# Two conv projections of a hybrid decoder layer as seven-product pairs behind attention

## The chip, the cores and the metric

One core of a Trainium2 chip runs the whole layer in one launch. The metric is device time in microseconds of that core; three runs of the kernel before gave 1265.51, 1268.23 and 1270.88 us. PE is the matmul engine (PEld its weight loads), DVE the vector engine, ACT the scalar engine, POOL is GpSimd, SP the engine that mostly issues transfers.

## The reference

One layer, 1024 positions of width 1024. `B`, `C`, `xc` are called cb, cc, cx in the kernel, 512 columns each; the gates are ga and gc, 1024 columns each.

```python
proj = h @ w_in[l]
q, k, v, cb, cc, cx, g_att, g_conv = jnp.split(proj, IN_SPLITS, axis=-1)
o = stick_breaking_attention(heads(q), heads(k), heads(v))
y_att = o.transpose(0, 2, 1, 3).reshape(b, s, ATT_WIDTH) @ w_att_branch[l]
y_conv = (cb * causal_dwconv(cc * cx, conv_mix_w[l])) @ w_conv_branch[l]
merged = jax.nn.sigmoid(g_att) * y_att + jax.nn.sigmoid(g_conv) * y_conv
x = x + rms_norm(merged @ w_out[l], norm_mix_post[l])
h = rms_norm(x, norm_ffn_pre[l])
u = causal_dwconv(h @ w_up[l], conv_ffn_w[l])
a, g = jnp.split(u, 2, axis=-1)
f = (jax.nn.gelu(g, approximate=True) * a) @ w_down[l]
x = x + rms_norm(f, norm_ffn_post[l])
```

Attention has 8 heads of 64. Its weight for query t and key s is sigmoid(z[t,s]) times the product of 1 - sigmoid(z[t,j]) for s < j < t, so each row needs a scan over the keys between the two matrix products.

## The kernel before, in words

**Numbers.** A float32 operand is held as two fp16 tiles, hi and lo, under a power-of-two scale. A product takes three matmuls (hi x hi, hi x lo, lo x hi; PASSES) for every 128 rows of depth. ACT makes the hi part (L102, L550), DVE the lo part (L103, L551). A scale needs a sum over all of the tile: squares on ACT (L63), a one-column matmul `pr` with ones on PE (L81, L475), and a few tiny DVE instructions.

**The first half of the run** is ordered by a planner (class Plan, L1826). Every piece of work is a job with engine, cost, the buffers it reads and writes, and a due time; the planner writes out an order for each of PE, DVE, ACT, SP and POOL. PE's backbone are the fills (list FILL, L33): v, then the projections q, k, cb, cc, cx (4 tiles of 128 columns each; 192 matmuls of 512 columns for each of the five), the first gate tiles ga0 and gc0, and four half-tiles of the conv branch (`branch_fill`). Attention work is put between pieces of the fills. Weights of a fill are loaded by POOL (L543), in buffers `ws`, and split into `wh`.

**Attention** is 48 units: per pair of heads j = 0 to 3 three groups of four units, two diagonal ones (keys and queries in the same half of the positions) and one that is not. A unit: z = q k (PE, L757, buffer z: 2), sigmoid into e (ACT, L778, buffer e: 3), two scans (DVE, L785), hi part of the weight w (ACT, L799, buffer w: 2), lo part (DVE, L805/L808), and two transposes of w into wt (SP, L796, hi and lo). After four units, eight transposes, `weigh` makes o = wt v on PE (24 matmuls, also L757). wt has one buffer, so the transposes of a group wait until o of the group before has read it. The names below are `z2_113`: pair of heads 2, query half 1, key half 1, block 3.

**Conv.** `conv_fill` evicts cc to u (ACT), multiplies u by cx on eviction (DVE, L690), takes the three taps (ACT L695, DVE L697), multiplies by cb (DVE, L690) and sums squares. `p_parts` splits the result p into p16 (L709, L710). All of it is a part of the plan, beside attention.

**Behind the plan** another scheduler keeps the order of the code on each engine, apart from a few evictions raised in priority. `branch` makes the conv branch y_conv tiles ywc (from p16 and wc) and the attention branch tiles ywa (from o16 and wa), 24 matmuls per tile of 128 columns (L886). `blocks(q)` makes sums and differences of the four quarters of h (T1 to T4, L919, L921, L923) and splits them into hB and a part of hT (`halves`, L909 on ACT, L910 on DVE). They feed the pairs: two weight tiles multiplied with h by seven block products instead of eight (class Pair; a product is 4 k x 3 matmuls, so 84 for two tiles where plain projection takes 96). `pair_fetch` loads the two tiles (SP, L119), `pair_sums` and `pair_split` form the weight combinations (L1060 to L1062, L1075) and split them into four `wh` tiles (L102, L103). Gate pairs g1 to g7 run so (L1954), with `merge_m` (L941, L943) multiplying gates and branches into m, and `split_m` splitting m under a scale that needs the sums of all 16 branch tiles (known at d = 3). Then come the out-projection (py, L1208) and the ffn (pu L1407, pq L1566, pd L1636 and L1669).

## Time and profile before

| | |
|---|---|
| runs | 1265.51, 1268.23 (median), 1270.88 us |
| profiled execution | 1263.36 us, span of its instructions 1261.6 us |
| granted PE clock | 0.998 |
| moved by the DMA engines | 152.43 MB |
| stages by the start of their first instruction on PE | o of the first group 72.1, last o 332.4, first gate pair 426.0, out-projection 554.4 us |

The profile is of one execution. A row by line gives line, engine, operation, output<-inputs by the program's names (buffer numbers left out), count, busy time, mean duration in ns, and the idle time of the engine ahead of it with what ended it. A matmul's duration runs from issue to end, and matmuls overlap, so the price of one is read from a stretch of them. A wait is put down to the instruction that ended it.

### The profile page before, as it was taken

The numbers are of one execution on the slowest core, as the hardware profiler recorded it, in microseconds if no ns is written. First come the engines' busy times: TensorE is split into PE (matmuls) and PEld (weight loads), VectorE is DVE, ScalarE is ACT, GpSimd is POOL, SyncE is SP. The second block draws the span as 40 slices with busy tenths as digits, with TensorE's granted clock in tenths as the row PEclk, the third lists the DMA queues.
The fourth block names the chain that finished last, engine by engine and source line by source line (L and its number), as shares of the span: only waits on it lengthen the run. The fifth ranks groups of instructions, "written<-read, shape, count | busy, mean of one in ns | idle before, by whom it ended". The sixth has DMA issues, their size and how long they took to land.

```text
span 1261.6 us, 16604 instructions
## 1 busy us (share of the span) xinstructions
PE 1244.5 (99%) x6120; PEld 562.6 (45%) x6120; DVE 1030.1 (82%) x1661; ACT 836.8 (66%) x1215; POOL 99.1 (8%) x137
## 2 busy tenths in 40 slices
PE   9999999999999999999999999999999999999997
PEld 4444444444444444444444444444444444444443
DVE  7977787468729658888889999799799979969976
ACT  7665666346559657765566759768876977878424
POOL 1200000000000000001100001001200300111003
PEclk9999999999999999999999999999999999999999
DMA  8854665535502113414952304614930971594608
GB/s 277 190 136 102 133 131 105 101 76 100 125 2 67 67 34 133 168 68 104 229 156 76 126 21 171 229 34 71 240 124 2 179 222 34 83 248 157 180 1 134
DMA packets 146628, 152.43 MB, mean 121 GB/s; under 512 B 114169, under 2 KB 114297, under 8 KB 146546
## 3 DMA queue, kind: packets, MB, share of 16 engines
q1 hardware_dynamic: 132720, 102.07, 29.7%
q0 software_dynamic: 13824, 49.29, 17.6%
q8 instruction: 48, 0.79, 0.3%
q14 instruction: 34, 0.28, 0.1%
q10 hardware_dynamic: 2, 0.00, 0.0%
HBM read 84.49 MB, written 37.75 MB: 97 GB/s over the span
## 4 chain that ended last, share of the span: by engine, by line
PE 45%; DVE 2%; DMA 1%; ACT 1%; issue 1%; POOL 1%; POOLq 0%; DVEq 0%; ACTq 0%
PE pq L1566 12%; PE pd L1636 2%; PE pd L1669 1%; DMA hB<-n 1%; PE pu7b L1407 1%; PE pu10b L1407 1%; PE pu9b L1407 1%; PE pu2b L1407 1%; PE pu20b L1407 1%; PE pu17b L1407 1%; PE pu15b L1407 1%; PE pu13b L1407 1%; PE pu6b L1407 1%; PE pu4b L1407 1%; PE pu21b L1407 1%
## 5 line engine op out<-in xcount | busy, mean ns | idle before, releaser
L1407 PEld LDWEIGHTS <-wh_u 128*128 128x128 f16 x1848 | 179.2, 98 | 218.6 <-issue 2.1
L1954 PEld LDWEIGHTS <-wh_g 128*128 128x128 f16 x588 | 56.9, 98 | 68.4
L1157 DVE SCALAR_TENSOR_TENSOR wh_u<-ws_u,sc_u,wh_u 128x1024 f16<-128x1024 f32 (+1 forms) x66 | 72.2, 1103 | 15.3 <-ACT wh_u L1155 14.7
L1155 ACT ACTIVATE wh_u<-ws_u,sc_u 128x1024 f16<-128x1024 f32 (+1 forms) x66 | 66.3, 1006 | 26.9 <-DVE sc_u L1140 5.5
L1208 PE MATMUL py<-wh_wo,m 128*128 128x512 f16 x384 | 83.6, 379 | 0.0
L1570 ACT ACTIVATE st<-pq,sd 128x512 f32<-128x512 f32 x112 | 73.6, 698 | 9.8 <-DVE ua L1450 5.6
L1121 POOL DMA_DIRECT2D acc<-st x56 | 43.9, 783 | 427.3 <-ACT st L1570 427.3
L63 ACT ACTIVATE jk_u<-ws_u 128x1024 bf16<-128x1024 f32 x44 | 46.3, 1052 | 22.7 <-DMA ws_u<-w_up_nt 22.4
L799 ACT ACTIVATE w<-e 128x1024 f16<-128x1024 f32 (+3 forms) x48 | 40.1, 837 | 31.6 <-DMA wt<-w 30.7
L1208 PEld LDWEIGHTS <-m 128*128 128x128 f16 x384 | 37.4, 98 | 44.9
L1439 DVE SCALAR_TENSOR_TENSOR ua<-ca,cw_a,ua 128x1023 f32<-128x1023 f32 (+1 forms) x44 | 56.2, 1278 | 1.2 <-ACT ua L1437 1.1
L1439 DVE SCALAR_TENSOR_TENSOR ug<-cg,cw_g,ug 128x1023 f32<-128x1023 f32 (+1 forms) x44 | 56.2, 1278 | 0.1
L778 ACT ACTIVATE e<-z,cz 128x1024 f32<-128x1024 f32 (+3 forms) x48 | 42.3, 896 | 21.0 <-PE z L757 10.5
L785 DVE TENSOR_TENSOR_SCAN e<-e,mask 128x512 f32<-128x512 f32 (+3 forms) x64 | 49.3, 810 | 5.6 <-ACT e L778 5.5
L564 PE MATMUL pq<-hT,wh_q 128*128 128x512 f16 x192 | 42.8, 379 | 1.4 <-DMA hT<-x 1.4
L564 PE MATMUL pcc<-hT,wh_cc 128*128 128x512 f16 x192 | 43.8, 379 | 0.0
L564 PE MATMUL pk<-hT,wh_k 128*128 128x512 f16 x192 | 43.7, 379 | 0.0
L564 PE MATMUL pcb<-hT,wh_cb 128*128 128x512 f16 x192 | 43.7, 379 | 0.0
L564 PE MATMUL pcx<-hT,wh_cx 128*128 128x512 f16 x192 | 43.6, 379 | 0.0
L785 DVE TENSOR_TENSOR_SCAN e<-e,cr,mask 128x512 f32<-128x512 f32 x32 | 39.6, 1271 | 4.1 <-ACT e L778 4.1
L1566 PE MATMUL pq<-wq,fx 128*128 128x512 f16 x192 | 42.8, 379 | 0.0
L1566 PE MATMUL pq<-wq,fy 128*128 128x512 f16 x192 | 42.7, 379 | 0.0
(733 smaller groups left out, 2750.6 us busy)
## 6 DMA issues: line engine op xcount, KB each, us to landing
acc<-st POOLq DMA_DIRECT2D x56, 512.0 KB, 5.9
ws_u<-w_up_nt SPq DMA_DIRECT2D x44, 512.0 KB, 3.8
ds<-w_down SPq DMA_DIRECT2D x22, 512.0 KB, 10.8
ws_g<-w_in_nt SPq DMA_DIRECT2D x14, 512.0 KB, 3.6
x<-x SPq DMA_DIRECT2D x8, 512.0 KB, 8.5
ws_wo<-w_out SPq DMA_DIRECT2D x8, 512.0 KB, 5.9
xr<-x SPq DMA_DIRECT2D x8, 512.0 KB, 4.2
yacc<-acc SPq DMA_DIRECT2D x16, 256.0 KB, 11.2
```

The costliest lines, as they stand in the source:

```text
L63: self.nc.scalar.activation(self.junk(f"jk_{name}"), src, AF.Square, accum_out=acc)
L564: pe.matmul(ps.t, w.t[:, wi, ds(k * P, P)], hT[:, hi, k, ds(c * NH, NH)], start=k == 0 and p == 0, stop=k == KD - 1 and p == 2)
L785: vec.tensor_tensor_scan(x, x, m[:, ::-1], ONE if diag else cr.t[:, h:h + 1], ALU.mult, ALU.max)
L1121: j = pl.add(eng, 0.45 if eng == "SP" else 1.14, lambda: e.dma_start(dst(), srcf(), **kw), r, [b] if w is None else w, ahead=AHEAD["load"] ...
L1155: A(C["As" if big else "Ash"], lambda: act.activation(dst.t[:, 0, dsl], src.t[:, ssl], AF.Copy, scale=sb.t["s"]), [(src, sreg), sb], [(dst ...
L1157: V(C["V" if big else "Vh"], lambda: vec.scalar_tensor_tensor(dst.t[:, 1, dsl], src.t[:, ssl], sb.t["s"], dst.t[:, 0, dsl], ALU.mult, ALU. ...
L1208: pe.matmul(b.t, m16[k].t[:, h_, ds(tt * P, P)], wo[k].t[:, w_, sl], start=k == 0 and p == 0, stop=k == 7 and p == 2)
L1407: pe.matmul(b.t, p.w[wt].t[:, wi, ds(wc * NH + k * P, P)], pr.block(i, h, k), start=first and n == 0, stop=n == 3 * KH - 1, skip_group_che ...
L1439: V(C["V"], lambda lag=lag: vec.scalar_tensor_tensor(u.t[:, lag:], c.t[:, :T - lag], sm.t[:, 2 - lag:3 - lag], u.t[:, lag:], ALU.mult, ALU ...
L1566: pe.matmul(b.t, fa[p].t[:, h, ds(fo * NH + tt * P, P)], wa[p].t[:, x, ds(wo * NH, NH)], start=first and n == 0, stop=n == 5, skip_group_c ...
L1570: A(C["Ah"], lambda tt=tt, b=b, st=st: act.activation(st.t[:, tt % 2, :], b.t, AF.Copy, scale=q.sd.t[:, 0:1]), [b, q.sd], [(st, str(tt % 2 ...
L1954: nc.tensor.matmul(ps, w[wt][:, wi, ds(wc * NH + k * P, P)], self.block(i, hi, k), start=first and n == 0, stop=n == 3 * KH - 1, skip_grou ...
```

## The change

- FILL keeps q, k, cc and the first gate tiles. cx and cb leave the plan and become four pairs x0, x1, b0, b1 (class Conv) of seven products each, between the attention branch and the gate pairs. `conv_taps` and `conv_gate` do what `conv_fill` did, on whole tiles of 1024 columns; `p_split` follows b1 at d = 1.
- All four wa tiles are loaded and split inside the plan; the eight wa branch tiles follow the plan at once, with blocks(0) ahead of them and blocks(1) after the fourth. T4 goes into hT at once.
- The wc tiles are loaded by POOL inside the plan for the sums of their squares only (one scale for all four) and loaded again by SP later; the wc branch tiles stand behind the first four gate pairs, two at each.
- The scale of m takes a bound for the wc part (from the scales of p and wc) in place of the sums of ywc, so m is split inside `merge` from d = 1.
- In attention, the weights w of even blocks t lie in the general slab (`slot`), those of odd t in the two old buffers: four in all.
- Of the units, those with c = 1 may start two fills later (4 + START).

```diff
-FILL = ("q0 k0 q1 k1 cc0 cx0 q2 k2 cb0 cc1 cx1 cb1 cc2 cx2 q3 k3 cb2 cc3 cx3 cb3 ga0 gc0").split()
+FILL = "q1 k1 cc0 q2 k2 q3 k3 cc1 cc2 cc3 ga0 gc0".split()
...
+        self.psrc.update({f"{n}{i}": [win[b + 2 * i], win[b + 2 * i + 1]] for n, b in (("x", 16), ("b", 8)) for i in range(2)})
...
-                    def conv_fill(j, which):
...
+                    def cc_fill(j):
+                        w, b = weight(f"cc{j}", win[12 + j])
+                        sm = Buf(None, lambda: self.small(f"cv{j}", keep=True))
+                        u = uf[j] = Buf("s", lambda: self.slot([P, T], F32, f"u{j}"))
+                        V(0.12, lambda: self.mul(sm.t[:, 0:1], inv_h, b.t["inv"]), [b, g_s], [sm])
...
-                    smpb, p16 = NOTE(), {}
-
-                    def p_parts():
-                        b = total("p", smpb, lambda: smp_, 4, True)
...
-                    def branch_fill(d):
...
-                        w16 = Buf("w", lambda: att.tile([P, 2, 2 * NH], F16, tag="w", name=f"w{nm}", bufs=2))
+                        w16 = Buf("w", lambda: att.tile([P, 2, 2 * NH], F16, tag="w", name=f"w{nm}", bufs=2)) if t % 2 else \
+                            Buf("s", lambda: self.slot([P, 2, 2 * NH], F16, f"w{nm}"))
...
-                            if "cz" not in s or (u["c"] and n < 2 + START):
+                            if "cz" not in s or (u["c"] and n < 4 + START):
...
-                    for i in (0, 1):
-                        W["wc", i] = weight(f"wc{i}", a["wc"][i])
+                    wa = [weight(f"wa{i}", a["wa"][i]) for i in range(4)]
+                    smw, wcb = self.small("sm_wc", keep=True), NOTE()
+                    for i in range(4):
+                        t = Buf("ws", lambda i=i: self.ws.tile([P, D], F32, tag="ws", name=f"wr_wc{i}"))
+                        j_ = pl.add("G", 1.14, lambda i=i, t=t: nc.gpsimd.dma_start(t.t, a["wc"][i]), [], [t], ahead=LOADS)
+                        j_.load, j_.lag = 1.45, 4.0
+                        A(1.2, lambda i=i, t=t: self.sumsq(t.t, smw[:, i:i + 1], f"wc{i}"), [t], [wcb], ahead=SQ)
+                    wcs = total("wc", wcb, lambda: smw, 4, True)
...
-                t4s.append(diff("T4", (kB, lo), t2, False))
                 t3 = diff("T3", (kB, hi), (kA, hi))
                 halves(hB[:, :, 2, ds(2 * q, 2), :], t3)
-
-            def branches(*ds_, bi=1):
-                for d in ds_:
-                    for _ in branch(bi, d, pm):
-                        pass
-
-            def merge_m(d):
+                t4 = diff("T4", (kB, lo), t2, False)
+                halves(hT[:, :, kA, hi], t4)
...
+            def wc_fetch(i):
+                t = self.ws.tile([P, D], F32, tag="ws", name=f"ws_wc{i}")
+                nc.sync.dma_start(t, a["wc"][i])
+                wc[i] = t
+
+            def wc_split(i):
+                w = self.wh.tile([P, 2, D], F16, tag="wh", name=f"wh_wc{i}")
+                self.split(w, wc[i], s_wc, f"wc{i}")
+                wc[i] = w
+
+            def wc_branch(d):
+                branch("wc", d, wc[d // 2], p16, sgn[:, 8:9], self.slot([P, T], F32, f"ywc{d}"))
...
+            def merge(d):
                 for which, yw in (("gc", "wc"), ("ga", "wa")):
                     y = ys[yw, d]
                     nc.vector.tensor_tensor(y, y, sig[which, d], ALU.mult)
...
                     self.slot([P, 2, T], F16, f"m16_{d}")
                 self.split(t, m, s_m, f"m{d}")
                 m16.append(t)
...
+            def conv_taps(p, i):
+                sm = self.small(f"cs{i}", keep=True)
+                self.mul(sm[:, 0:1], inv_h, p.inv)
+                for j, x in ((2 * i, p.ca), (2 * i + 1, p.cg)):
+                    u, q = uf[j], self.o16p.tile([P, T], F32, tag="o16", name=f"pf{j}")
+                    nc.vector.scalar_tensor_tensor(u, x, sm[:, 0:1], u, ALU.mult, ALU.mult)
+                    nc.scalar.activation(q, u, AF.Copy, scale=self.cmw[:, j, 2:3])
+                    for lag in (1, 2):
+                        nc.vector.scalar_tensor_tensor(q[:, lag:], u[:, :T - lag], self.cmw[:, j, 2 - lag:3 - lag], q[:, lag:],
+                                                       ALU.mult, ALU.add)
+                    pf[j] = q
+
+            def conv_gate(p, i):
+                sm = self.small(f"cb{i}", keep=True)
+                self.mul(sm[:, 0:1], inv_h, p.inv)
+                for j, x in ((2 * i, p.ca), (2 * i + 1, p.cg)):
+                    nc.vector.scalar_tensor_tensor(pf[j], x, sm[:, 0:1], pf[j], ALU.mult, ALU.mult)
+                    self.sumsq(pf[j], smp_[:, j:j + 1], f"p{j}")
+
+            def p_split():
+                s, inv = self.scale_of(smp_, 4, keep=True)
+                self.mul(sgn[:, 8:9], inv, inv_wc)
+                nc.vector.tensor_scalar(smy[:, 8:9], sgn[:, 8:9], 2.0 ** 28, None, ALU.mult)
+                self.mul(smy[:, 8:9], smy[:, 8:9], smy[:, 8:9])
+                nc.vector.tensor_scalar(smy[:, 0:9], smy[:, 0:9], 2.0, None, ALU.mult)
+                s_m, inv_m = self.scale_of(smy, 9, keep=True)
+                for j in range(4):
+                    x = self.slot([P, 2, T], F16, f"p16_{j}")
+                    self.split(x, pf[j], s, f"p{j}")
+                    p16.append(x)
+                return s_m, inv_m
...
-            branches(0, 1, bi=0)
-            with tc.issue_after(last[0].ins):
-                blocks(0)
-            branches(2, 3, bi=0)
...
+            seq = ["x0", "x1", "b0", "b1"] + [f"g{d}" for d in range(1, 8)] + ["u0"]
+            at = seq.index("g1") - 1
+            blocks(0)
+            for d in (0, 1, 2, 3):
+                wa_branch(d)
             blocks(1)
-            branches(0, 1, 2, 3)
-            for q in range(2):
-                halves(hT[:, :, ds(2 * q, 2), NH:], t4s[q])
-            self.pair_sums("g1")
-            self.pair_split("g1")
-            self.pair_fetch("g2")
-            branches(4, 5)
-            self.pair_sums("g2")
-            ms = [merge_m(0)]
-            self.hA, self.hB = hT, hB
-            gp = {d: Gates(self, f"g{d}") for d in range(1, 8)}
+            self.pair_fetch("x0")
+            for d in (4, 5):
+                wa_branch(d)
+            self.pair_sums("x0")
+            self.pair_split("x0")
+            self.pair_fetch("x1")
+            for d in (6, 7):
+                wa_branch(d)
+            self.pair_sums("x1")
...
+            prs = [(Gates if n[0] == "g" else Conv)(self, n) for n in seq[:-1]]
+            last = len(prs) - 1
+            for n, p in enumerate(prs):
+                name, d = seq[n], n - at
                 p.prod(1)
+                if n:
+                    q = prs[n - 1]
+                    q.prod(4)
+                    if seq[n - 1][0] == "g":
+                        sig["gc", d - 1], sig["ga", d - 1] = q.ca, q.cg
+                if n < last:
+                    self.pair_split(seq[n + 1])
+                    self.pair_fetch(seq[n + 2])
+                if n and seq[n - 1][0] in "xb":
+                    (conv_taps if seq[n - 1][0] == "x" else conv_gate)(q, int(seq[n - 1][1]))
+                if d == 1:
+                    s_m, inv_m = p_split()
+                    wc_fetch(0)
...
-                    if d >= 4 and i == 5:
-                        split_m(d - 1, ms[d - 1])
...
+                if n < last:
+                    self.pair_sums(seq[n + 2])
+                if 0 < d < 5:
+                    wc_split(d - 1)
+                    if d < 4:
+                        wc_fetch(d)
+                    wc_branch(2 * d - 2)
+                    wc_branch(2 * d - 1)
+                if d == 1:
+                    merge(0)
...
-                    s_m, inv_m = self.scale_of(smy, 16, keep=True)
-                    for i in range(3):
-                        split_m(i, ms[i])
...
+class Conv(Pair):
+
+
+    def out(self, name):
+        return self.l.xp.tile([P, T], F32, tag="x", name=name)
+
+    def c11(self, dst, ps):
+        self.nc.scalar.activation(dst, ps, AF.Copy)
```

**SP around the last attention group, before.** The wt3_103 rows are the transposes of the last group, ws_ rows weight loads.

```order
L796 DMA_TRANSPOSE wt3_113_2933<-w3_111_3002 128x4x128 x2
L796 DMA_TRANSPOSE wt3_113_2933<-w3_110_3041 128x2x128 x2
L796 DMA_TRANSPOSE wt3_103_3130<-w3_103_3044 128x8x128 x2
L796 DMA_TRANSPOSE wt3_103_3130<-w3_102_3092 128x8x128 x2
L119 DMA ws_wa0_0_3554<-wa 128x1024
L796 DMA_TRANSPOSE wt3_103_3130<-w3_101_3168 128x8x128
L796 DMA_TRANSPOSE wt3_103_3130<-w3_100_3192 128x8x128
L796 DMA_TRANSPOSE wt3_103_3130<-w3_101_3168 128x8x128
L796 DMA_TRANSPOSE wt3_103_3130<-w3_100_3192 128x8x128
L119 DMA ws_wa1_0_3559<-wa 128x1024
L119 DMA ws_wa2_0_3564<-wa 128x1024
L119 DMA ws_wa3_0_3569<-wa 128x1024
```

And now:

```order
L684 DMA_TRANSPOSE wt3_113_2541<-w3_111_2494 128x4x128
L684 DMA_TRANSPOSE wt3_113_2541<-w3_110_2526 128x2x128
L119 DMA ws_x0_0_3027<-w_in_nt 128x1024
L684 DMA_TRANSPOSE wt3_103_2698<-w3_103_2608 128x8x128
L684 DMA_TRANSPOSE wt3_103_2698<-w3_102_2618 128x8x128
L684 DMA_TRANSPOSE wt3_103_2698<-w3_103_2608 128x8x128
L684 DMA_TRANSPOSE wt3_103_2698<-w3_102_2618 128x8x128
L684 DMA_TRANSPOSE wt3_103_2698<-w3_101_2659 128x8x128 x2
L684 DMA_TRANSPOSE wt3_103_2698<-w3_100_2711 128x8x128 x2
L119 DMA ws_x0_1_3031<-w_in_nt 128x1024
L119 DMA ws_x1_0_3125<-w_in_nt 128x1024
L119 DMA ws_x1_1_3129<-w_in_nt 128x1024
```

The wa loads are gone from SP; the load of x0's first tile stands ahead of the last group's eight transposes, and the other pair loads follow them.

**DVE behind its last instruction of attention, before.** w3_100 is the last weight tile; pf, p and s0p belong to conv, wh_wc is a split of wc.

```order
L805 SCALAR_TENSOR_TENSOR w3_100_3192<-e3_100_3079,w3_100_3192 128x1024
L690 SCALAR_TENSOR_TENSOR pf3_3160<-pcb3_1_3182,cv3_2496,pf3_3160 128x512
L467 TENSOR_REDUCE s0p_3245<-sm_p_110 128x1
L468 CAST rb_p_3246<-s0p_3245 128x1
L551 SCALAR_TENSOR_TENSOR wh_wc3_0_3243<-ws_wc3_0_3081,sc_wc3_3189,wh_wc3_0_3243 128x1024
L94 TENSOR_SCALAR s0p_3245<-pr_p_3256 128x1
L96 TENSOR_SCALAR s0p_3245<-s0p_3245 128x1
L97 TENSOR_SCALAR s0p_3245<-s0p_3245 128x1
L106 TENSOR_TENSOR sgn_108<-s0p_3245,sc_wc2_3075 128x1
L106 TENSOR_TENSOR sgn_108<-s0p_3245,sc_wc3_3189 128x1
```

And now:

```order
L693 SCALAR_TENSOR_TENSOR w3_100_2711<-e3_100_2651,w3_100_2711 128x1024
L495 SCALAR_TENSOR_TENSOR wh_wa2_0_2687<-ws_wa2_0_2404,sc_wa2_2556,wh_wa2_0_2687 128x1024
L495 SCALAR_TENSOR_TENSOR wh_wa3_0_2738<-ws_wa3_0_2499,sc_wa3_2653,wh_wa3_0_2738 128x1024
L94 TENSOR_SCALAR s0wc_2726<-pr_wc_2742 128x1
L96 TENSOR_SCALAR s0wc_2726<-s0wc_2726 128x1
L97 TENSOR_SCALAR s0wc_2726<-s0wc_2726 128x1
L780 TENSOR_TENSOR T1_0_2856<-hT_90 128x1024
L782 TENSOR_TENSOR T1_0_2856<-T1_0_2856,hT_90 128x1024
L784 TENSOR_TENSOR T1_0_2856<-T1_0_2856,hT_90 128x1024
L780 TENSOR_TENSOR T2_0_2862<-hT_90,T1_0_2856 128x1024
L780 TENSOR_TENSOR T3_0_2867<-hT_90 128x1024
L782 TENSOR_TENSOR T2_0_2862<-T2_0_2862,hT_90 128x1024
```

The eviction of cb and the scale of p gave place to splits of wa and to the blocks of h (T1_0 to T3_0), which stood at row 396 and later.

**POOL in attention, before.** Each row is one weight load.

```order
L543 DMA ws_cb0_0_1231<-w_in_nt 128x1024
L543 DMA ws_cc1_0_1373<-w_in_nt 128x1024
L543 DMA ws_cx1_0_1513<-w_in_nt 128x1024
L543 DMA ws_cb1_0_1635<-w_in_nt 128x1024
L543 DMA ws_cc2_0_1770<-w_in_nt 128x1024
L543 DMA ws_cx2_0_1909<-w_in_nt 128x1024
L543 DMA ws_q3_0_2032<-w_in_nt 128x1024
L543 DMA ws_k3_0_2180<-w_in_nt 128x1024
L543 DMA ws_cb2_0_2284<-w_in_nt 128x1024
L543 DMA ws_cc3_0_2399<-w_in_nt 128x1024
```

And now, from the same row number on:

```order
L487 DMA ws_k3_0_1242<-w_in_nt 128x1024
L487 DMA ws_cc1_0_1388<-w_in_nt 128x1024
L487 DMA ws_cc2_0_1536<-w_in_nt 128x1024
L487 DMA ws_cc3_0_1667<-w_in_nt 128x1024
L487 DMA ws_ga0_0_1821<-w_in_nt 128x1024
L487 DMA ws_gc0_0_1953<-w_in_nt 128x1024
L745 DMA wr_wc0_2114<-wc 128x1024
L745 DMA wr_wc1_2202<-wc 128x1024
L487 DMA ws_wa0_0_2295<-wa 128x1024
L487 DMA ws_wa1_0_2307<-wa 128x1024
L487 DMA ws_wa2_0_2404<-wa 128x1024
L487 DMA ws_wa3_0_2499<-wa 128x1024
```

Loads of cx and cb are gone; wc (twice needed, here for its sums) and wa come behind gc0. Over the whole program POOL has 137 rows before and 133 now, SP 265 and 288, PE 6110 matmuls and 6055.

209 lines of the change are left out of this document (43 added, 166 removed).

## The prediction

> **What bounds the kernel now.** I read the page first: which engine fills the span.
>
> ```profile
> span 1261.6 us, 16604 instructions
> PE 1244.5 (99%) x6120; PEld 562.6 (45%) x6120; DVE 1030.1 (82%) x1661; ACT 836.8 (66%) x1215; POOL 99.1 (8%) x137
> PEclk9999999999999999999999999999999999999999
> ```
>
> PE is busy for 1244.5 of 1261.6 us at a full clock in every slice, so only fewer matmuls, or fewer of the remaining 17.1 us of idle time, can shorten the run. The waits of PE (line, releaser: total, times, longest) say how little idle time there is to win:
>
> ```profile
> PE z L757 <- ACT e L778: 2.0, 3, 1.0
> PE warm L374 <- DVE wz L289: 1.7, 1, 1.7
> PE pq L564 <- DMA hT<-x: 1.4, 1, 1.4
> PE pu0a L1407 <- ACT cg L1416: 1.2, 1, 1.2
> PE o L757 <- DMA wt<-w: 1.2, 2, 1.0
> ```
>
> Two of these belong to attention (z waits for the ACT sigmoid, o for the transposed weights): 3.2 us. The table by stage shows why it is so little. Columns: stretch, its length, busy time of PE, PEld, DVE, ACT, POOL, clock, DMA share, GB/s. The stretches are: ten of the twelve attention groups; the wc and wa branches with the blocks of h; four gate pairs; a part of the ffn.
>
> ```profile
> 105.80:335.20 229.40, 226.27 (x1307) 98.83 (x1305) 166.80 (x289) 128.13 (x181) 9.01 (x17) 1.00 0.56 115
> 335.20:422.10 86.90, 86.90 (x411) 39.45 (x410) 58.25 (x89) 61.78 (x94) 0.00 (x0) 1.00 0.14 46
> 466.20:554.40 88.20, 88.20 (x415) 40.04 (x414) 69.64 (x123) 63.28 (x95) 1.06 (x2) 1.00 0.37 132
> 700.00:800.00 100.00, 100.00 (x468) 45.38 (x467) 93.50 (x134) 74.22 (x102) 7.51 (x14) 1.00 0.32 111
> ```
>
> Attention's latency is hidden because projections fill PE between its units. Behind it PE never waits in these stretches, even where DVE is 93.5% busy.
>
> **What the change takes from PE.** The price of a matmul of 512 columns comes from the chain that ended last, in a piece where matmuls run back to back:
>
> ```profile
> 772.33 15.56 PE pq L1566 x72
> ```
>
> 15.56 / 72 = 0.216 us. As fills, cx and cb take 4 tiles x 2 halves x 24 = 192 matmuls each, 384 in all. As pairs, two tiles take 7 products x 4 k x 3 passes = 84 instead of 96, so four pairs take 336. That is 48 x 0.216 = **10.4 us less**. Seven one-column products for scales go as well; one costs the 0.03 us between these two starts, 0.2 us together:
>
> ```profile
> 471.37 0.17 PE L81 MATMUL pr<-rb,ones 128*128 128x1 bf16 x1
> 471.40 0.81 PE L1954 MATMUL pg3b<-hB,wh_g 128*128 128x512 f16 x3
> ```
>
> PE's sum is -10.6 us. Everything else can only give some of it back, since the wc and wa branches, gates, out-projection and ffn keep their matmuls. The new scale of m and the fourth w buffer remove no wait of PE: none of the rows above is theirs, so I count both at nothing.
>
> **Attention, with less cover.** These projections leave it (columns: count, then busy time, mean ns of one from issue to end):
>
> ```profile
> L564 PE MATMUL pcb<-hT,wh_cb 128*128 128x512 f16 x192 | 43.7, 379 | 0.0
> L564 PE MATMUL pcx<-hT,wh_cx 128*128 128x512 f16 x192 | 43.6, 379 | 0.0
> ```
>
> 384 x 0.216 = 82.9 us leave the stretch of ten groups. The last product o moves forward in the fill list too: it now stands in gc0, behind 18 ga, 30 gc and 3 wa matmuls that came after it, 51 x 0.216 = 11.0 us of new cover. So PE has 226.3 - 82.9 + 11.0 = 154.4 us of work for ten groups, 15.4 each where it had 22.6.
>
> What must fit under that is the chain through wt, which has one buffer: eight transposes of a group cannot start until o of the group before has read it. Rows of tile wt (duration min/median/max in ns, then issue to landing in us), of SP's wait for that buffer, and two products o:
>
> ```profile
> L796 SPq DMA_TRANSPOSE wt<-w x96: 1168/1267/3240, 56.0 to 325.4; - x96
> DMA to landing us min/median/max: 2.3/3.3/6.1
> SPq L796 <- PE o L757: 50.6, 10, 15.0
> 141.54 1.82 PE L757 MATMUL o<-wt,v 128*64 128x512 f16 x24
> 124.67 2.78 PE L757 MATMUL o<-wt,v 128*64 128x512 f16 x24
> ```
>
> SP waited 50.6 us for PE to free the buffer: slack of the chain, and the change takes 72 us out of the same stretch. One turn of the chain is seven issues, the landing L of the eighth, and o (1.82 us for a diagonal group, 2.78 otherwise): 7 x 1.267 + L + 1.82 = 10.7 + L, or 11.65 + L. Counting matmuls between the o's in the changed order, at these prices, gives PE 12.6, 14.1, 14.5, 14.2, 13.0 and 14.1 us for the diagonal turns and 16.4 to 19 for the other four. With L at the median 3.3 a diagonal turn takes 14.0: PE waits 1.4 + 1.0 = 2.4 us in two groups. With L = 2.3 it waits 0.4, with L = 4.8 it waits 10.4, and with the longest, 6.1, 19.6 (18.3 in the six diagonal turns, 1.3 in the shortest other one). I take L = 3.8: the median, and half a microsecond because the loads that POOL issues (17 in the stretch before, some 13 now in two thirds of the time) share DMA engines that were 0.56 busy. That gives (14.5 - 12.6) + 0.4 + 0 + 0.3 + 1.5 + 0.4 = **+4.5 us** (0.4 to 19.6). The Trainium skill, page "DMA: Bandwidth & Descriptors", section "Issuing engines are not separate DMA queues", says that transfers started from SP and from GpSimd run on the same 16 DMA engines and interleave; the spread of 2.3 to 6.1 us agrees, and by it L is no constant here.
>
> z waits for e (2.0 us before) may grow too, but of DVE's 166.8 us in the old stretch the evictions, taps and splits of cx and cb go too; I leave that in the ends of the range.
>
> **From the wa branches to pair x0.** The blocks of h stood in 87 us, with wc branches ahead of wa. Now 189 matmuls of wa and 18 of gc are all that PE has between the last o and x0: 207 x 0.216 = 44.7 us. DVE's rows for that time:
>
> ```profile
> L921 DVE TENSOR_TENSOR T<-T,hT 128x1024 f32<-128x1024 f32 x8 | 9.7, 1220 | 0.1
> L910 DVE TENSOR_TENSOR hB<-T,hB 128x1024 f16<-128x1024 f32 x6 | 7.3, 1217 | 23.5 <-ACT hB L909 23.5
> L923 DVE TENSOR_TENSOR T<-T,hT 128x1024 f32<-128x1024 f32 x4 | 4.9, 1220 | 0.1
> L919 DVE TENSOR_TENSOR T<-hT,T 128x1024 f32<-128x1024 f16 x4 | 4.9, 1219 | 0.1
> L919 DVE TENSOR_TENSOR T<-hT 128x1024 f32<-128x1024 f16 x4 | 4.9, 1217 | 0.0
> L910 DVE TENSOR_TENSOR hT<-T,hT 128x1024 f16<-128x1024 f32 x2 | 2.4, 1218 | 0.0
> ```
>
> Together 34.1 us. Splits and sums of x0 are those of a gate pair:
>
> ```profile
> L103 DVE SCALAR_TENSOR_TENSOR wh_g<-ws_g,sc,wh_g 128x1024 f16<-128x1024 f32 x14 | 17.8, 1280 | 4.7 <-ACT wh_g L102 4.7
> L1061 DVE TENSOR_TENSOR s_g<-s_g,ws_g 128x512 f32<-128x512 f32 x7 | 4.8, 687 | 0.1
> ```
>
> Three large ones at 1.28, a half one and four half-wide sums at 0.69 make 7.3; with wh_wa2 and wh_wa3 (2.6) and a multiply (1.2) DVE has 45 us to do. It begins after its last w low, which stands at least an issue, a landing and o, 7.4 us, ahead of the end of the last o, so it has 52 us; but hB waits for ACT (23.5 us before, hidden then), and ACT has 16 evictions and 8 sums of wa in between. On SP the load of ws_x0_0 now stands ahead of the last group's eight transposes and waits for the split wh_wa1. In DVE's order that split is the first large one after w3_102, so it is done before o has freed wt unless DVE is late; if it is, the eight transposes and the last o wait with it. Together **+1.5 us** (0 to 7). The cover is the 44.7 us of wa and gc; without it the blocks' 34 would show.
>
> **p16 in the first gate pair.** The four splits of p now come just ahead of their first product in ywc0, which the order mixes with pg1.
>
> ```profile
> L710 DVE SCALAR_TENSOR_TENSOR p<-pf,s0p,p 128x1024 f16<-128x1024 f32 x4 | 4.9, 1281 | 2.0 <-ACT p L709 2.0
> ```
>
> Four at 1.28 us behind conv_gate's sums: **+0.5 us** (0 to 3). Conv's taps and gates cost DVE the same instructions as before, now beside the pairs:
>
> ```profile
> L697 DVE SCALAR_TENSOR_TENSOR pf<-u,cmw,pf 128x1022 f32<-128x1022 f32 x4 | 5.1, 1283 | 0.1
> ```
>
> An x pair costs DVE 7.3 of splits and sums, 3.5 for five evictions at 0.69 and six operations of 1.28 on u and pf, 18.5 us beside 84 x 0.216 = 18.1 us of PE; a b pair has two such operations, 13.4. The four have 64 us beside 72.6. wc branches stretch the gate pairs to 28 us each, so merges, splits and SP's 23 more issues (pair loads and the reload of wc, fetched a pair ahead) are covered: nothing.
>
> **Sum.** -10.6 + 4.5 + 1.5 + 0.5 = -4.1 us on the profiled execution's 1263.36 us: 1259.3. The median of the runs shown, 1268.23, is 4.9 us above that execution, which is shorter than any of the three; -4.1 on the median is **1264 us**. A difference of 0.5%, 6.3 us, is about what a measurement of this kernel can tell from no change.
>
> **Rivals.** A, full cover: the transposes land near the minimum and the wa matmuls hide the blocks; then all 10.6 us stay, 1257.6 us. For it: 3.2 us of waits in attention, and ffn slices at 93.5% DVE without a wait. Against it: two diagonal turns are shorter than the chain at the median L. B, the saving is eaten: L of about 4.8 costs 10.4 and x0 waits up to 7 for hB; net 0 to +6, 1268 to 1274. For it: hB's 23.5 us wait for ACT. C, the other side: the wt chain becomes attention's bound. If L averages 6.1, seven of the ten turns are late, 19.6 us, and with 1.5 from the transition it is -10.6 + 21.1 = +10.5 us, 1278.7; the kernel is slower by over 6.3 us from L of about 5.5. For it: 6.1 has been measured, and transposes of 3.24 us; against it: 3.3 is the median under a DMA share of 0.56. The Trainium skill, page "Perfetto Trace Analysis", section "Optimization Strategy", says that interleaving regimes with different busiest engines can help; the change takes such interleaving apart, so by that rule the run gets slower, as in C. The trace before agrees with the rule only in so far as PE, with the projections mixed in, lost 3.2 us in attention. That the change does not do what it says is excluded: the order has 336 matmuls where 384 stood.
>
> **Chances.** Forecast (net -8 to -1) 0.50, of which 0.17 below -6.3; A 0.21; B 0.17; C 0.12. Faster by over 0.5%: 0.17 + 0.21 = 0.38. Within: 0.33 + 0.16 = 0.49. Slower: 0.12 and 0.01 of B, 0.13. The range runs from A's end, 1257, to B's, 1274, and leaves out C and a little below A.
>
> **What would show it.** The out-projection's first matmul of before:
>
> ```profile
> 554.40 0.38 PE L1208 MATMUL py<-wh_wo,m 128*128 128x512 f16 x1
> ```
>
> Right: PE has 336 matmuls in px and pb, waits "o <- DMA wt" of 3 to 6 us in total, the last o near 335 - 72 + 5 = 268 us, and this row starts about 4 us earlier. Wrong for A's sake: no new wait of PE between 100 and 270 us. Wrong for B or C: waits of o or z over 10 us, or of px0 for hB or wh_x0 over 3 us. DVE over 95% busy in attention, with z waiting for e, would be a cause that I have not priced.

## The result and the profile after

On one chip the kernel before took 1267.24 us (median of 10 runs, 1263.01 to 1273.17) and the changed one 1276.25 us (10 runs, 1272.51 to 1285.06). The ratio is 1.0073, 95% interval 1.0048 to 1.0099: slower, and outside the range of the prediction (1257 to 1274). The profiled executions are 1263.36 and 1276.38 us, 13.0 us apart. Times below are of profiled executions, medians and ratios apart.

The page of the changed kernel, first lines:

```profile
span 1274.7 us, 16496 instructions
PE 1238.9 (97%) x6065; PEld 560.6 (44%) x6065; DVE 1051.2 (82%) x1669; ACT 841.7 (66%) x1219; POOL 96.6 (8%) x133
```

PE's busy time fell by 5.6 us only, not by 10.6, and its idle time rose from 17.1 to 35.8 us: -5.6 + 18.7 = +13.1. PE's waits of the changed kernel (line, releaser: total, times, longest) say where:

```profile
PE o L644 <- issue: 5.5, 2, 5.0
PE pcc L508 <- ACT u L624: 4.5, 1, 4.5
PE pu2a L1338 <- ACT hb L1268: 2.3, 1, 2.3
PE o L644 <- DMA wt<-w: 2.0, 3, 0.9
PE z L644 <- ACT e L666: 2.0, 2, 1.5
PE py L1139 <- ACT wh_wo L102: 1.8, 1, 1.8
...
```

Attention has 5.5 + 4.5 + 2.0 + 2.0 = 14.0 us where it had 3.2 (+10.8), and two single waits make 9.5 of it. Further down the list, gate pair g1 has 0.8 + 0.7 + 0.5 = 2.0 (pg1b, pywc, pg1c); the start of the out-projection has 1.8 + 0.7 = 2.5 (py, pg7c), the start of the ffn 2.3 + 1.0 = 3.3 (pu2a, pt). That is 18.6 of the 18.7 us. The stretch of ten groups (length; busy PE, PEld, DVE, ACT, POOL; clock; DMA share; GB/s):

```profile
106.69:278.08 171.39, 157.22 (x967) 68.64 (x968) 137.56 (x240) 105.41 (x155) 7.39 (x14) 0.97 0.74 151
```

The last o ends at 278.08, not near 268. The clock, 1.00 before, is 0.97 here; it is 0.83 from 110 to 130 us and 0.91 from 230 to 250, around the two long waits. Run e1 below has the same 967 matmul records in this stretch at a clock of 1.00, and PE is busy 153.33 us there: the slow clock costs 157.22 - 153.33 = 3.9 us. That is most of the 5.0 us that PE's busy time has too much; 0.8 of the rest lie ahead of these groups (102.50 us for 514 matmul records, before 101.68), and no run tells why. The pieces behind the two waits (columns as above) show the same, 0.42 x 4.68 + 0.43 x 3.99 = 3.7 us:

```profile
125.38:130.06 4.68, 4.68 (x25) 2.31 (x26) 0.61 (x2) 0.00 (x0) 0.00 (x0) 0.58 0.01 4
238.51:242.50 3.99, 3.99 (x14) 1.10 (x14) 3.92 (x10) 3.97 (x8) 0.43 (x1) 0.57 0.01 2
```

**The first long wait.** PE's timeline (start, duration, instruction, idle before and releaser) has an o whose cause the view cannot name ("issue"); tile wt and POOL's timeline can:

```profile
125.38 4.69 PE L644 MATMUL o<-wt,v 128*64 128x512 f16 x24 [5.02 <-issue]
```

The eight transposes of that turn (duration of the issue min/median/max in ns, start of the first and of the eighth issue; then issue to landing, the end of the transfer, of all eight, and of the eighth alone):

```profile
L684 SPq DMA_TRANSPOSE wt<-w x8: 1262/1360/3627, 106.7 to 122.1; - x8
DMA to landing us min/median/max: 3.2/5.5/10.0
```

```profile
DMA to landing us min/median/max: 3.2/3.2/3.2
```

The eighth landed 3.2 us after its issue, at the 3.3 us that is the median of all 96, before and now. It was issued late: from the first issue to the eighth passed 15.4 us. Seven issues of 1.267 us are 8.9, and run e1, without the loads, took 9.6 here:

```profile
L684 SPq DMA_TRANSPOSE wt<-w x8: 1261/1306/1342, 105.4 to 115.0; - x8
```

The landing of 10.0 us is that of the fifth transpose and ended ahead of the eighth's. POOL's timeline has the loads:

```profile
110.11 0.53 POOL L487 DMA_DIRECT2D ws_k<-w_in_nt  x1 [20.94 <-DVE wh_cc L495]
111.90 0.53 POOL L487 DMA_DIRECT2D ws_cc<-w_in_nt  x1 [1.26 <-DVE wh_q L495]
113.10 0.53 POOL L487 DMA_DIRECT2D ws_cc<-w_in_nt  x1 [0.67 <-DVE cz L106]
```

Three loads of 512 KB start within 3 us of each other, between the transposes of that turn. They come together because each waits for a split to free its load buffer, and DVE now runs the three splits close behind each other (each load starts 0.3 us after the end of a split; for the third the view names cz, a one-column instruction that follows the split):

```profile
108.54 1.28 DVE L495 SCALAR_TENSOR_TENSOR wh_cc<-ws_cc,sc_cc,wh_cc 128x1024 f16<-128x1024 f32 x1
...
110.33 1.27 DVE L495 SCALAR_TENSOR_TENSOR wh_q<-ws_q,sc_q,wh_q 128x1024 f16<-128x1024 f32 x1
111.52 1.28 DVE L495 SCALAR_TENSOR_TENSOR wh_k<-ws_k,sc_k,wh_k 128x1024 f16<-128x1024 f32 x1
```

Before, POOL's timeline over attention has the loads apart, all but one pair of them 11 to 16 us; the first three of 17:

```profile
105.99 0.53 POOL L543 DMA_DIRECT2D ws_cc<-w_in_nt  x1 [15.64 <-DVE wh_cx L551]
110.50 0.53 POOL L543 DMA_DIRECT2D ws_cx<-w_in_nt  x1 [3.98 <-DVE wh_q L551]
126.57 0.53 POOL L543 DMA_DIRECT2D ws_cb<-w_in_nt  x1 [15.54 <-DVE wh_k L551]
```

**The second** is not o. PE waits for an eviction that stands behind another wait on ACT (rows of PE, then ACT):

```profile
238.51 2.72 PE L508 MATMUL pcc<-hT,wh_cc 128*128 128x512 f16 x6 [4.49 <-ACT u L624]
```

```profile
236.10 1.79 ACT L687 ACTIVATE w<-e 128x1024 f16<-128x1024 f32 x2 [4.55 <-DMA wt<-w]
237.79 0.67 ACT L624 ACTIVATE u<-pcc,cv 128x512 f32<-128x512 f32 x1
```

ACT must write w, whose buffer a transpose still reads; the eviction u, which frees a bank of the memory that PE writes to, is queued behind it. Here a landing is late: of this turn's eight transposes one takes 7.1 us, in e1 4.6 at most. Three more loads had started at 222.18, 223.30 and 229.80.

```profile
L684 SPq DMA_TRANSPOSE wt<-w x8: 1239/1337/1897, 226.2 to 236.8; - x8
DMA to landing us min/median/max: 2.4/4.8/7.1
```

**The out-projection.** ACT before, then now:

```profile
550.60 1.15 ACT L102 ACTIVATE wh_wo<-ws_wo,sc 128x1024 f16<-128x1024 f32 x1 [1.36 <-DVE sc L85]
```

```profile
560.97 1.15 ACT L102 ACTIVATE m<-ywa,sc 128x1024 f16<-128x1024 f32 x1 [2.55 <-DVE ywa L837]
562.03 1.13 ACT L102 ACTIVATE wh_wo<-ws_wo,sc 128x1024 f16<-128x1024 f32 x1
```

The split of m6 (m of the pair d = 6), possible earlier since the scale of m comes from a bound, now stands ahead of the first split of wo, which PE's next matmul needs; before, m's split stood behind it.

### The profile page after: what moved, and what is told of

Its sections match the earlier page's. It is cut to its first block, busy times and chain, and to the rows that moved or that the text cites. A ratio compares the mean times of both kernels' runs of the same rounds, so it can differ in the third digit from the quotient of the medians.

```text
span 1274.7 us, 16496 instructions
## 1 busy us (share of the span) xinstructions
PE 1238.9 (97%) x6065; PEld 560.6 (44%) x6065; DVE 1051.2 (82%) x1669; ACT 841.7 (66%) x1219; POOL 96.6 (8%) x133
## 4 chain that ended last, share of the span: by engine, by line
PE 44%; DVE 2%; ACT 1%; issue 1%; DMA 1%; POOL 1%; POOLq 0%; DVEq 0%; ACTq 0%
PE pq L1497 11%; PE pd L1567 2%; PE pd L1600 1%; PE pu7b L1338 1%; PE pu20b L1338 1%; PE pu17b L1338 1%; PE pu15b L1338 1%; PE pu13b L1338 1%; PE pu10b L1338 1%; PE pu9b L1338 1%; PE pu6b L1338 1%; PE pu4b L1338 1%; PE pu2b L1338 1%; PE pu21b L1338 1%; PE pu19b L1338 1%
## 5 line engine op out<-in xcount | busy, mean ns | idle before, releaser
L1501 ACT ACTIVATE st<-pq,sd 128x512 f32<-128x512 f32 x112 | 74.0, 697 | 10.4 <-DVE ua L1381 5.6
L666 ACT ACTIVATE e<-z,cz 128x1024 f32<-128x1024 f32 (+3 forms) x48 | 42.1, 896 | 14.6 <-PE z L644 11.9
L804 PE MATMUL pywc<-p,wh_wc 128*128 128x512 f16 x192 | 43.1, 379 | 0.7 <-DVE p L103 0.7
L1497 PE MATMUL pq<-wq,fs 128*128 128x512 f16 x192 | 42.1, 379 | 0.0
L804 PE MATMUL pywa<-o,wh_wa 128*128 128x512 f16 x192 | 41.8, 379 | 0.0
```

Of the source, the lines that this page charges most:

```text
L804: nc.tensor.matmul(ps, wt[:, wi, ds((d % 2) * NH + k * P, P)], x[k][:, hi, ds(c * NH, NH)], start=n == 0, stop=n == 11)
L1497: pe.matmul(b.t, fa[p].t[:, h, ds(fo * NH + tt * P, P)], wa[p].t[:, x, ds(wo * NH, NH)], start=first and n == 0, stop=n == 5, skip_group_c ...
L1501: A(C["Ah"], lambda tt=tt, b=b, st=st: act.activation(st.t[:, tt % 2, :], b.t, AF.Copy, scale=q.sd.t[:, 0:1]), [b, q.sd], [(st, str(tt % 2 ...
```

## The experiments

Theory: what the lost cover (PE's work that runs beside the chain) costs is set by the few turns in which loads come in a burst and delay transposes; each long wait is paid twice, as idle time and as slow clock; the small waits behind attention take the rest. Rivals: the thinner cover costs this by itself, whatever the loads do (the turn of seven issues, landing and o is simply longer than PE's work); or the saving of the pairs is not real. Each ratio is against the kernel before on the same chip:

| run | what | median us | ratio | 95% |
|---|---|---|---|---|
| e1_noloads | changed, no POOL loads | 1260.56 | 0.9952 | 0.9932 to 0.9971 |
| e8_before_noloads | before, no POOL loads | 1259.00 | 0.9935 | 0.9912 to 0.9958 |
| e10_noloads_repaired | e1, two orders repaired | 1255.16 | 0.9912 | 0.9885 to 0.9940 |
| e6_spread | three loads later | 1273.35 | 1.0051 | 1.0025 to 1.0077 |
| e5_wo | m6's split later | 1277.13 | 1.0092 | 1.0064 to 1.0120 |
| e7_both | e5 and e6 | 1269.25 | 1.0026 | 1.0000 to 1.0052 |
| v2_all | e7 and p split in parts | 1268.03 | 1.0021 | 1.0006 to 1.0035 |
| e9_w2 | two w buffers | 1299.08 | 1.0247 | 1.0208 to 1.0285 |
| e4_cb | only cb as pairs, two w buffers | 1269.64 | 1.0028 | 1.0007 to 1.0049 |
| v1_cb | e4, three repairs | 1273.93 | 1.0064 | 1.0052 to 1.0076 |
| v1w4_cb | v1_cb, four w buffers | 1298.19 | 1.0265 | 1.0230 to 1.0300 |
| v8_cb | e4, other repairs | 1269.53 | 1.0030 | 1.0005 to 1.0054 |

**e0_clock: what a wait of PE costs after it has ended.** The layer is left out; bursts of LONG = 72 matmuls follow gaps that DVE makes, each the longer the greater g is (GAPS = 0, 2 to 8, 10). The next burst needs x.

```diff
+            for rep in range(3):
+                for g in GAPS:
...
+                    for n in range(LONG):
+                        nc.tensor.matmul(ps, w, x, start=n == 0, stop=n == LONG - 1)
...
+                    for _ in range(g):
+                        nc.vector.tensor_scalar(big[:, :NH], big[:, :NH], 1.0, None, ALU.mult)
...
+                    nc.vector.tensor_copy(x, big[:, :NH])
```

> This kernel leaves out the whole layer: it runs bursts of 72 matmuls of 512 columns (15.6 us at 0.216) with idle gaps of PE between them, from under 1 to about 7 us, three times over, and writes a constant. In the changed kernel two idle times of 5.0 and 4.5 us were each followed by slower matmuls (24 products o took 4.69 us where others take 2.78) and a lower granted clock. If the idle time itself lowers the clock, bursts behind gaps of 4 us and more start slow by 2 to 3 us and bursts behind gaps under 2 us do not. If the slow matmuls came from something else in attention (the transposes' traffic, say), all bursts here take the same 15.6 us.

PE's timeline, the gap in brackets:

```profile
57.76 15.71 PE L66 MATMUL ps<-x,w 128*128 128x512 f16 x72 [2.10 <-DVE x L71]
76.03 17.40 PE L66 MATMUL ps<-x,w 128*128 128x512 f16 x72 [2.56 <-DVE x L71]
...
160.36 18.37 PE L66 MATMUL ps<-x,w 128*128 128x512 f16 x72 [4.41 <-DVE x L71]
```

Gaps up to 2.10 us cost nothing more; 2.56 to 3.95 cost 1.6 to 1.7; 4.41 and 5.33 cost 2.7 to 2.8, alike in all three repetitions. A window in the burst behind the gap of 2.56 us (PE, PEld, DVE, POOL, clock):

```profile
77.30:78.60 1.30, 1.30 (x5) 0.46 (x4) 0.00 (x0) 0.00 (x0) 0.50 0.00 0
```

The loss is time at half clock: 2 x 1.7 = 3.4 us, or 2 x 2.7 = 5.4. So an idle time is enough to lower the clock, with no transposes about. Its price does not carry over as it stands: by e0 the changed kernel's waits of 5.02 and 4.49 us would cost 2.7 each, 5.4 us, and they cost 3.9. The Trainium skill, page "TensorE: Matmul & The Clock Gate", section "What's actually happening", says that a hardware monitor halves the clock after an idle window of about 3.4 us and that the window runs freely. The half clock and the 3.4 us agree; a gap of 2.56 us, shorter than that window, already cost it here.

**e1_noloads and e8_before_noloads: attention without POOL's loads.** The weights that POOL loads are filled with a constant instead; buffers, waits and order stay. The same edit in both kernels (a part of one line; in the changed one also at its four loads of wc):

```diff
-lambda: nc.gpsimd.dma_start(t.t, src)
+lambda: nc.gpsimd.memset(t.t, 0.01)
```

> The changed kernel, but the weight loads that POOL issues are replaced by a fill of the same buffers with a constant on POOL: the projections q1 to gc0 and wa then use constant weights. The order on PE, DVE, ACT and SP is the same. Theory 'loads': the two long waits of PE in attention (5.0 and 4.5 us) come from loads that land in bursts among the transposes; without loads PE waits under 4 us in attention in all, its clock stays at 1.00, transposes land in under 4 us, and the time falls by 12 to 16 us to 1260 to 1264 us (0.994 to 0.998 of before). Rival 'cover': with 15.4 us of PE work for a group the chain through the one wt buffer and the latency of the units do not fit whatever the loads do; PE still waits 8 us or more in attention and the ratio to before stays over 1.002.

> The kernel before, with POOL's weight loads replaced by a fill with a constant, as in e1_noloads. There the loads cost the changed kernel 15 us. Theory: under the old cover of 22.6 us a group the same loads cost next to nothing, only the waits of o and z (3.2 us): ratio 0.997 to 1.000. Rival: the loads cost either kernel about the same (by the start of the run, for one), and the ratio is 0.99 or less; then the cover is not what the change took away.

Of e1, tile wt, the ten groups, and PE's longest wait:

```profile
DMA to landing us min/median/max: 2.3/3.1/4.6
```

```profile
105.38:261.59 156.21, 153.33 (x967) 66.72 (x968) 137.15 (x240) 105.96 (x155) 13.32 (x14) 1.00 0.62 119
```

```profile
PE py L1139 <- ACT wh_wo L102: 2.5, 1, 2.5
```

No transpose takes over 4.6 us to land (under 4 was expected). The stretch is 15.2 us shorter at full clock, with the same 967 matmul records and the same work on DVE; attention's waits are 3.3 us (pcc 1.5, o 1.6, z 0.2). So thin cover alone does not cost it: it takes the loads as well. They cost the kernel before too, more than expected but less than the changed one: 1 - 0.9935 is 8 us (6.1 by the medians of that chip, 1265.07 and 1259.00), and 1.0073 / 0.9952 = 1.012 is 15. Without them the medians differ by +1.6 us, not +9, which the overlapping intervals do not tell from zero, and still not by -10.6: a second cause stands behind attention.

**e10_noloads_repaired: that second cause.** e1, with two orders repaired: the split of m6 behind the first step of wo (e5's edit), and one of the four splits of p behind each of the first products of g1 instead of all four ahead (`p_split` no longer splits p).

```diff
-                s_m, inv_m = p_split()
+                s_m, inv_m, s_p = p_split()
...
                     p.prod(i)
+                    if d == 1 and len(p16) < 4:
+                        p_part(len(p16), s_p)
```

> The changed kernel without POOL's weight loads (e1_noloads: constant weights) and with the splits of m6 and p placed as in v2_all. The kernel before without these loads had ratio 0.9935 and the changed one 0.9952, so even without loads the 10.6 us of matmuls were lost elsewhere. Theory: 2.5 us of that and 1.7 us of lower clock are the output weights, 1 to 2 us g1, the rest waits of units in attention (3.3) and the ffn's start; repaired, the ratio is 0.990 to 0.993, under that of the kernel before without loads. Rival: the saved matmuls are worth less than counted, or the waits move; then the ratio stays at 0.994 or over.

The median is 1255.16 us, 5.4 below e1's and 3.8 below e8's, and no run of e10 (1256.32 at most) is as long as the shortest of e8 (1257.94). The page's PE row, of e8 and then of e10:

```profile
PE 1243.5 (99%) x6120; PEld 561.9 (45%) x6120; DVE 1029.8 (82%) x1661; ACT 836.4 (67%) x1215; POOL 109.4 (9%) x137
```

```profile
PE 1233.4 (98%) x6065; PEld 558.3 (45%) x6065; DVE 1051.6 (84%) x1669; ACT 841.4 (67%) x1219; POOL 106.1 (8%) x133
```

Here the saving stands in the open: 1243.5 - 1233.4 = 10.1 us of PE. Of it 3.1 go to attention (pcc, o, z), where e8 has no wait, and 5.0 to hb, pg2b, pg1b and pt; 1.8 come back at pu0a (2.2 in e8, 0.4 here): 3.8 are left, and the spans differ by 4.2. The waits for wh_wo and p are gone.

**e6_spread, e5_wo, e7_both, v2_all: the same repairs with the loads in place.** e6 holds POOL back ahead of three loads, so that no two fall together in the first turn; nothing moves on PE, DVE, ACT or SP. e5 moves m6's split. e7 is both, v2 also has p's splits in parts.

```diff
+LATER = {"cc1": 10, "cc2": 3, "wa2": 5}
...
+for _ in range(LATER.get(name, 0)):
+    nc.gpsimd.memset(t.t, 0.0)
 nc.gpsimd.dma_start(t.t, src)
```

```diff
-                self.split(t, m, s_m, f"m{d}")
+                if d != 6:
+                    self.split(t, m, s_m, f"m{d}")
...
+                    if d == 7 and i == 5:
+                        self.split(m16[6], ys["wa", 6], s_m, "m6")
```

> The changed kernel with every load kept, but three of POOL's weight loads come later: cc1 by about 10 us, cc2 by 3 more, wa2 by 5 (the buffer is filled with zeros some times before its load). All other engines keep their order. Theory 'loads in bursts': behind the first wait of 5.0 us stand k3, cc1 and cc2 issued within 3 us; with one load instead of three beside the transposes of that group the wait falls under 2 us and the slow matmuls behind it go (2.7 us), the second wait (4.5 us) falls by about 2; 6 to 9 us less than the changed kernel, ratio to before 1.000 to 1.003. If it is the volume of the loads and not their time, the waits move to the following groups and the ratio stays at 1.006 to 1.009.

> The changed kernel, but the split of m6 stands behind the first step of the split of the output weights, as it did before. PE lost 1.8 + 0.7 us there at the first product of the out-projection. If the order on ACT is the cause, both waits go, and the time falls by about 2.5 us against the changed kernel (ratio to before 1.005). If the output weights themselves come later (their loads land in 7.2 us where 5.9), the wait stays.

> The later loads of e6_spread together with the split of m6 behind the first step of the output weights (e5_wo). Theory: both gains add, e6_spread less about 1.5 us; ratio 0.998 to 1.002. If the waits of PE there only move, the ratio is that of e6_spread.

> The whole change, with the later loads and the later split of m6 (e7_both) and the splits of p spread over g1. Theory: the 2.0 us of waits in g1 fall under 1, ratio 1.000 to 1.002, still not under the kernel before, since attention keeps some 11 us of waits of z and o and the lower clock behind those over 2.3 us. If it is 0.997 or less, the loss was behind attention rather than in it.

e6's o of the first long wait, and its waits:

```profile
121.27 2.78 PE L649 MATMUL o<-wt,v 128*64 128x512 f16 x24 [1.54 <-issue]
```

```profile
PE z L649 <- ACT e L671: 3.4, 4, 1.6
PE o L649 <- DVE e L678: 2.5, 1, 2.5
...
PE o L649 <- issue: 2.2, 2, 1.5
...
PE o L649 <- DMA wt<-w: 2.0, 2, 1.5
...
PE pcc L513 <- ACT u L629: 1.6, 1, 1.6
```

With cc1 and cc2 later the first wait falls from 5.02 to 1.54 us (the seven issues take 11.9 us), no slow clock is left in attention in this execution, and PE is busy 1235.8 us. But the waits of attention still sum to 11.7 us: the time won at the long waits is partly waited out again at shorter ones. That is what e6's rival, the volume of the loads, had expected, and the ratio lies between the two forecasts. So the burst is shown as the cause of the first long wait and of the clock behind it; that bursts alone set what the lost cover costs is not shown. In e6's twelve runs the clock is 0.994 to 0.998, so some of them still have slow stretches somewhere. The interval of e6's ratio overlaps the changed kernel's, so the 3 us between their medians are not settled by the time alone; the wait itself is. e5 alone brings no gain in time (1.0092), although its wait for wh_wo fell from 1.8 to 1.0 and pg7c's went; the pair e6 and e7 differs by 0.25% the other way. What that repair is worth with the loads in place stays open. e5, e6 and e7 all came out above the ratios expected. v2_all, the whole change with all repairs, is 0.5% below the changed kernel, at the upper edge of its expectation, but is still not faster than before.

These executions also show that the price of a wait is not a matter of its length alone. In e7 a wait of 2.00 us (and one of 1.50 at 134.10 us) was followed by half clock; in e6 one of 2.45 was not (row of the wait, then the clock behind it, columns as above):

```profile
216.17 1.31 PE L649 MATMUL z<-k,q 64*128 64x512 f16 x12 [2.00 <-ACT e L671]
218.00:220.00 2.00, 2.00 (x6) 0.46 (x3) 2.00 (x4) 2.00 (x4) 0.00 (x0) 0.50 0.67 129
```

```profile
251.94 1.82 PE L649 MATMUL o<-wt,v 128*64 128x512 f16 x24 [2.45 <-DVE e L678]
252.20:254.20 2.00, 2.00 (x28) 1.45 (x25) 0.48 (x4) 1.81 (x3) 0.00 (x0) 1.00 0.04 10
```

**e9_w2: two w buffers again.** The edit gives w two buffers for all tiles, as before the change; the planner then orders attention anew.

```diff
-w16 = Buf("w", ..., bufs=2) if t % 2 else Buf("s", lambda: self.slot([P, 2, 2 * NH], F16, ...))
+w16 = Buf("w", ..., bufs=2)
```

> The changed kernel with two buffers for the attention weights, as before, and not four. The second long wait runs through ACT's write of w, which waits for a transpose to release its buffer. Theory: with two buffers ACT waits for transposes in every group; PE waits 5 to 15 us more in attention, ratio 1.011 to 1.02. Rival: the buffers were not needed, since the one wt buffer limits the transposes anyhow, and the ratio stays at 1.005 to 1.010.

```profile
PE o L644 <- DMA wt<-w: 17.3, 2, 13.4
```

1.0247 / 1.0073 = 1.017, 22 us slower than the changed kernel and more than expected; z waits another 15.0 us for e. So the kernel with the old buffers loses more. How much of it is the buffers and how much the new order was not separated, and v1w4_cb below, where four buffers are the slower, warns against crediting the buffers with it.

**e4_cb, v1_cb, v1w4_cb, v8_cb: half of the change.** e4 keeps cx in attention and makes only cb a pair. v1 repairs the m6 and p orders in it and makes the scale of wc behind the plan; v1w4 is v1 with four w buffers; v8 keeps that scale in the plan, behind the last o. The remarks behind # in the second piece are not code.

```diff
-FILL = "q1 k1 cc0 q2 k2 q3 k3 cc1 cc2 cc3 ga0 gc0".split()
+FILL = "q1 k1 cc0 cx0 q2 k2 cc1 cx1 cc2 cx2 q3 k3 cc3 cx3 ga0 gc0".split()
...
-seq = ["x0", "x1", "b0", "b1"] + [f"g{d}" for d in range(1, 8)] + ["u0"]
+seq = ["b0", "b1"] + [f"g{d}" for d in range(1, 8)] + ["u0"]
```

```diff
-wcs = total("wc", wcb, lambda: smw, 4, True)             # v1: dropped
+wcs = total("wc", wcb, lambda: smw, 4, True, [o16b[3]])  # v8
...
+s_wc, inv_wc = self.scale_of(smw, 4, keep=True)          # v1: ahead of pair b0
```

> Half of the change: cx goes back among the fills of attention, with its taps; only cb runs as pairs (b0, b1) behind it. Two buffers for the attention weights as in the kernel before; the rest as changed. PE gets 24 x 0.216 = 5.2 us less than before instead of 10.4, and attention keeps 41.5 us more cover, about 19.5 us a group. Theory 'cover' and theory 'loads' both expect waits in attention near those of before (3 to 5 us), so -5.2 + 1 + 4.5 (what the end of the gates and the start of the ffn lost) = 0: ratio 0.998 to 1.001. If the loss lies elsewhere (behind attention, in the pairs), the ratio stays over 1.004.

> cb alone as pairs (e4_cb), with three repairs behind attention: the split of m6 behind the first step of the output weights; the four splits of p one behind each product of g1 and not all ahead; the scale of wc made behind the plan, so that no sum product stands among the last attention products (PE waited 2.5 us for it in e4_cb and its clock fell). Theory: 5.2 us of matmuls saved stay saved once these waits go: e4_cb was 3.5 us over the kernel before; less 3 for the output weights, 4 for the sum product and its clock, 1.5 for g1 gives 5 us under it, ratio 0.994 to 0.999. Rival 'cover': any loss of cover in attention costs what it saves; then the waits move and the ratio stays at 1.000 to 1.003.

> v1_cb with the four buffers for the attention weights of the change, and not two. If the buffers help in themselves, as the loss of 25 to 35 us without them in e9_w2 says for the thin cover, it is as fast as v1_cb or up to 2 us faster; with 19.5 us of cover a group the two should be equal within 0.2%.

> cb alone as pairs (e4_cb) with three repairs: the split of m6 behind the first step of the output weights, the splits of p one behind each product of g1, and the sum product of wc's scale behind the last attention product (it stays in the plan, unlike in v1_cb, where the order around g1 changed with it and PE waited 4.5 and 3.1 us there). Theory: e4_cb's 3.5 us over the kernel before less 3 (output weights), 4 (sum product and clock) and 1: 4 us under it, ratio 0.994 to 0.999. If waits only move, 1.000 to 1.003.

All four missed. The longest new wait of e4, then of v1; then waits of v8:

```profile
PE pr_wc L419 <- DVE rb_wc L412: 2.5, 1, 2.5
```

```profile
PE pr L81 <- DVE rb L76: 4.5, 1, 4.5
```

```profile
PE z L661 <- ACT e L682: 3.7, 3, 1.9
PE o L661 <- DMA wt<-w: 3.7, 3, 2.1
```

With cx as cover, attention's waits for o (0.6) and z (1.4) are 2.0 us, less than the 3.2 before, although a transpose takes up to 9.3 us to land: the thicker cover has room for it. e4's largest new wait is at one small product for the scale of wc, which stands in PE's order ahead of its operand. In v8 that wait is gone and PE is busy 3.3 us less (1242.4 to 1239.1), but z and o wait 7.4 us. In v1 and v8 the repairs moved the order, and waits opened elsewhere. Why four w buffers make v1 24 us slower was not followed up.

## Why the prediction was wrong

- **The products**: right. -10.6 was forecast; PE lost 10.1 us of busy time between e8 and e10, at granted clocks of 0.998 and 0.999.
- **"Attention, with less cover"**: the step that failed. PE's work for the ten groups was right: 154.4 us forecast, 153.33 in e1. The chain set against it was not. The term was +4.5 (0.4 to 19.6); measured were +10.8 of waits and 3.9 of slow clock, 14.7. That is inside the term's own range, but the range of the whole ended with rival B, which has 10.4 for it.
- What was mis-sized in it for the first long wait: the term "7 x 1.267". The sum held the issues of a turn constant and put all doubt into the landing L of the eighth transpose. In the late turn L was 3.2 us, and the issues took 15.4 instead of 8.9. The prediction's own row had single issues of 3.24 us. In the other turns the waits for o come to 2.5 us together. That the loads would come in a burst could be read from DVE's order: they wait for the splits, and with cx and cb gone three splits stand together. What the Trainium skill says on this, page "DMA: Bandwidth & Descriptors", section "Issuing engines are not separate DMA queues", that transfers of all issuers interleave, the runs bear out (a transpose landed after up to 10.0 us with the loads, 4.6 without).
- The same step knew one chain, through wt. The second long wait went through the buffers of w and ACT's queue, where an eviction for PE stood behind. And it priced a wait at its length, with nothing for the clock; behind the two long waits that was 3.9 us.
- **Rival C** had the direction (0.12): transposes that land late make attention the bound. Its form, L of 6.1 in all turns, was not what happened. The rule of the Trainium skill that it named (page "Perfetto Trace Analysis", section "Optimization Strategy") came true in direction: with the interleaving taken apart the run took 1.0073 of the time. But without POOL's loads e10, as much taken apart, is 3.8 us faster than e8, so taking it apart does not cost by itself.
- **"From the wa branches to pair x0"**, +1.5 (0 to 7): no wait of px0, 0.
- **"p16 in the first gate pair"**, +0.5 (0 to 3): 2.0 with what follows in g1.
- **"Merges, splits and SP's issues: nothing"** and **"the new scale of m: nothing"**: +2.5 at the out-projection, since the scale lets m6's split pass ahead of wo's on ACT; with the order of before (e5) 1.0 of it was left. Only PE's waits before had been looked at, not ACT's order.
- **"The fourth w buffer: nothing"**: it removes no wait of the kernel before, but with two buffers and the order that follows from them the change is slower still (e9).
- **The start of the ffn** was not in the sum: +3.3. The waits for hb (1.0 to 2.3 us) are in every run of the whole change and not among the waits of before. No run tells their cause, and it stays open.

The sum with measured terms: -10.6 + 14.7 + 0 + 2.0 + 2.5 + 3.3 = +11.9. The other 1.1 us of the 13.0 that the profiled executions differ by are PE's busy time outside the ten groups, which stays unexplained.

## What to carry to other kernels

When work that covers a latency is taken away, look for the turn in which most things coincide and price that one, every issue of it and not only the last landing; a median over all turns hides it. Price the ordinary turns as well: with the burst spread (e6), 11.7 of the 14.0 us of waits in attention were still there. Loads that are released by one engine's instructions come as close together as those instructions do, so read that engine's order, and the order of every in-order queue that a moved step passes. A wait of PE can cost more than its length, since the clock may drop behind it; look at the granted clock behind each wait.

## What the hardware showed unexpectedly

- In bursts, a gap of PE of 2.10 us cost nothing afterwards, one of 2.56 us 1.7 us, one of 4.41 us 2.7 us, at a granted clock of 0.50. In attention a wait of 2.00 us was followed by a clock of 0.50 (e7) and one of 2.45 us by 1.00 (e6).
- Beside three loads of 512 KB within 3 us, a transpose took up to 10.0 us from issue to landing, and up to 3.63 us to issue; without the loads the longest were 4.6 and 2.19. The issue times, and not the last landing, made the turn of the first long wait late.
- The kernel before, too, is 6 us (by medians) to 8 us (by the ratio) faster without POOL's loads, though its profile shows only 3.2 us of waits in attention; with loads its ten runs spread over 10.2 us, without them eight spread over 2.4.
